# Experts of a decoder layer: running sums on GpSimd, another order of the experts, gathers that skip the padding

## The chip, the cores and the metric

The kernel runs on one core of a Trainium2 chip. Its metric is the device time of one execution in microseconds, as the median of several runs. The engines are TensorE (PE), VectorE (DVE), ScalarE (ACT), GpSimd (POOL) and SyncE (SP); SP issues the loads of weights and lists, GpSimd the indirect gathers and scatters. Times inside an execution are microseconds from the start of its span.

## The reference

One decoder layer for 2048 tokens of 1024 channels: a mixer sub-layer of three head groups, then a sub-layer of experts, then a final RMS norm. Only the experts and the final norm matter here. Each token goes to two of 32 experts (the best of 4 groups, and the two best of its 8 experts), and each expert is a SwiGLU of hidden width 512:

```python
def hier_moe(h, wg, bg, we, be, w_gate, w_up, w_down):
    ...
    weights = grp_p * jax.nn.softmax(top_l, axis=-1)
    expert = grp_i * MOE_EXPERTS_PER_GROUP + top_j
    ...
    def run(inp):
        xb, e = inp
        hid = jax.nn.silu(xb @ w_gate[e]) * (xb @ w_up[e])
        return hid @ w_down[e]
    ...
    contrib = out[dest] * flat_w[order][:, None].astype(out.dtype)
    y = jnp.zeros((T, D), out.dtype).at[tok_sorted].add(contrib)
...
    x = x + gt2 * hier_moe(h, ...)
return rms_norm(x, final_norm_g)
```

## The kernel before

The experts are the last stage of the program, from about 1900 us on. The routing has written, for each expert, a list of its tokens to DRAM (`tab_d`). The experts are worked off as 32 items in an order that the device finds: experts are ranked by how many rows they got, and the item at position p takes the expert of a rank that the list `CAP` stands for. `CAPR` holds the rows set aside for each rank (240, 208, 208, 208, 192, ... 88; 4644 in all, while the routing fills 4096), and `CAP` deals them out to positions:

```python
CAP = [CAPR[p // 2] if p % 2 == 0 else CAPR[31 - p // 2] for p in range(NE)]
```

So even positions hold the large items, falling from 240, and odd ones the small, rising from 88. An item of more than 128 rows is "full": its rows lie in two tiles (of half of them each), and it is computed with weights and inputs split in two parts (`wh`, `wl`: L1907 on ScalarE, L1908 on VectorE), gate and up in two halves of the hidden width (c = 0 and 1, L1957 and L1959), each ended by `ga` (a copy by ScalarE, L1963, and a sum by VectorE, L1964, for each of two PSUM banks m) and by `hid` (L1968, L1969). An item of up to 128 rows is "few": one tile, gate and up as plain fp32 matmuls on unsplit weights (L1931), then four transposes and `hid` (L1941). 18 items are full, 14 few. Positions 0 to 27 alternate (full, few), and the last four are full.

For an item r the program writes, in this order: the first half of gate and up of r (or all of it, if few); `finish` of item r - 2 (the product L2017 and the scatter L2018 to the output); `partial` of r - 1 (the gathers L1992 of what other experts have so far added to the rows, `part`); the first transposes of r + 1's rows (L1884, with `xT`, L1888 and L1889); the gathers L1866 of the rows of r + 2 (`xg`); the down projection of r - 1 (L162 to L164, with its eviction `y`, L1983); the rest of the transposes; the second half of r; and `add` of r - 1: the sum y + part (L2001), its scatter back to DRAM (L2004, `yp_d`), and the final norm's Square (L2009, ScalarE), `sx` (L2010) and a square root in 14 small steps (L61 to L67, VectorE). The sum carries a manual dependency, "products first": it stands behind the last `hid` product of item r in the scheduler's order.

The final rows go out through L2018 from whichever expert comes last for a token; a row index past the last token makes a scatter skip the row. All indirect gathers and scatters are issued by GpSimd, in the order in which they stand on it. A scheduler sets the order on each engine from the program, with a model of its own; within an engine the order is then fixed. Weights come in pieces of 512 KB through 11 buffers (`wraw`), a few item takes eight of them at once.

## Time and profile before

| | us |
|---|---|
| median of 3 runs | 2964.74 (2964.41 to 2969.07) |
| the profiled execution | 2962.22 |
| its span, first to last instruction | 2960.3 |
| mean granted TensorE clock | 0.886 of full speed |

Over the whole span TensorE is busy 2385.6 us (81%), VectorE 2103.6, ScalarE 1346.8 and GpSimd 1010.4. The experts' stage is the last third. Rows of a profile read: start and duration, engine, line of the kernel, operation, output <- inputs, and in brackets how long the engine had stood idle before and what released it. In rows of groups, busy time and mean duration in ns stand behind the bar, then the idle time before them and what ended it.

### The profile page before, as it was taken

What the parts mean: (1) busy time and instruction counts of PE and PEld (TensorE: products, weight loads), DVE (VectorE), ACT (ScalarE), POOL (GpSimd) and SP (SyncE); (2) the same over time, 40 slices, a digit from 0 to 9 for tenths busy, and PEclk for the clock granted to TensorE, in tenths of its full rate; (3) what the DMA queues carried; (4) which work ended last, traced back from release to release, by engine and by line L of the source; (5) the groups of instructions that cost most, each with busy time, mean ns of one, the idle gap of its engine ahead of it and who ended that gap; (6) DMA issues with size and microseconds to landing.
All of it is one profiled execution on the core that took longest, in us unless ns stands there. A gap on an engine that the chain in (4) does not pass through costs nothing. (4 is left out here: it accounts for less than half of the span.)

```text
span 2960.3 us, 38558 instructions
## 1 busy us (share of the span) xinstructions
PE 2385.6 (81%) x12571; PEld 1857.5 (63%) x12571; DVE 2103.6 (71%) x4776; ACT 1346.8 (45%) x2339; POOL 1010.4 (34%) x755
## 2 busy tenths in 40 slices
PE   3989877777567899858897999488889888987894
PEld 3766645776456677646675878465566655655673
DVE  6478867999978854547786566656667766666785
ACT  2568867574122244356665222244444444443452
POOL 2221133436635332155544344213222222323222
PEclk9999967898767979969998999699999989989997
DMA  7222254433331244243323443588888888887871
GB/s 217 86 92 85 79 200 156 112 136 124 106 106 54 83 147 137 67 149 111 112 69 123 152 148 123 151 271 251 263 272 269 258 250 265 253 247 235 260 226 36
DMA packets 372278, 479.41 MB, mean 162 GB/s; under 512 B 84827, under 2 KB 271355, under 8 KB 371813
## 3 DMA queue, kind: packets, MB, share of 16 engines
q1 hardware_dynamic: 334501, 421.83, 45.0%
q0 software_dynamic: 37568, 55.05, 7.0%
q8 instruction: 100, 1.64, 0.2%
q14 instruction: 109, 0.89, 0.1%
HBM read 385.75 MB, written 112.23 MB: 168 GB/s over the span
## 5 line engine op out<-in xcount | busy, mean ns | idle before, releaser
L1908 DVE TENSOR_TENSOR wl<-wraw,wh 128x1024 fp32r<-128x1024 f32 x272 | 329.6, 1221 | 187.0 <-ACT wh L1907 179.1
L1907 ACT ACTIVATE wh<-wraw 128x1024 fp32r<-128x1024 f32 x272 | 286.4, 1055 | 330.9 <-PE pd L164 120.6
L1957 PE MATMUL pg<-xT,wh 128*128 128x416 f32 (+10 forms) x1152 | 324.3, 361 | 18.6 <-DVE xT L1889 11.5
L1931 PE MATMUL pg<-wraw,xT 128*120 128x512 f32 (+9 forms) x448 | 231.0, 679 | 88.1 <-DVE ga__18823 L1964 11.1
L1959 PE MATMUL pg<-xT,wl 128*128 128x208 f32 (+10 forms) x1152 | 283.2, 246 | 0.0
L441 POOL TENSOR_TENSOR xx<-xr,xx 128x1024 fp32r<-128x1024 f32 x64 | 162.7, 2545 | 268.8 <-ACT xx L440 254.7
L1957 PEld LDWEIGHTS pg<-xT,wh 128*128 128x128 f32 x1152 | 223.2, 194 | 24.8 <-DVE xT L1889 14.0
L1931 PEld LDWEIGHTS pg<-wraw,xT 128*120 128x120 f32 (+9 forms) x448 | 88.2, 202 | 222.3 <-issue 120.3
L1959 PEld LDWEIGHTS pg<-xT,wl 128*128 128x128 f32 x1152 | 226.6, 197 | 0.4
L255 DVE SCALAR_TENSOR_TENSOR sb<-rl,iws,sb 128x1024 f32<-128x1024 f32 (+7 forms) x154 | 186.6, 1212 | 33.3 <-ACT rl L254 24.9
L2004 POOL DMA_INDIRECT yp_d<-y,ix x50 | 97.6, 1952 | 309.6 <-DVE y L2001 170.3
L162 PE MATMUL pd<-wh,hid 128*104 128x512 f32 (+17 forms) x400 | 164.8, 412 | 28.2 <-DVE y L1983 15.1
L162 PE MATMUL pp<-xx,w 128*128 128x256 f32 x512 | 153.5, 300 | 22.3 <-ACT ft L487 11.9
L254 ACT ACTIVATE rl<-pi,iwa 128x1024 f32<-128x1024 f32 (+7 forms) x176 | 157.0, 910 | 30.7 <-DVE sb L255 27.7
L163 PE MATMUL pd<-wl,hid 128*104 128x512 f32 (+17 forms) x400 | 161.1, 403 | 0.0
L164 PE MATMUL pd<-wh,hid 128*104 128x512 f32 (+17 forms) x400 | 160.7, 407 | 0.0
L163 PE MATMUL pp<-xx,w 128*128 128x256 f32 x512 | 151.2, 296 | 4.1 <-POOL xx L441 4.1
L164 PE MATMUL pp<-xx,w 128*128 128x256 f32 x512 | 150.3, 295 | 1.9 <-DVE w L177 1.1
L251 PE MATMUL pi<-iks,iqs 128*128 128x512 f32 (+3 forms) x304 | 110.4, 446 | 32.2 <-ACT rl L254 31.2
L162 PE MATMUL pj<-w,xx 128*128 128x512 f32 (+1 forms) x256 | 99.6, 390 | 40.2 <-DVE ot L208 18.9
L1538 DVE CUSTOM_DVE_ANT_0 pr<-ps,mk 128x512 f32<-128x512 f32 (+3 forms) x160 | 94.3, 605 | 47.6 <-PE ps L1537 28.4
L1992 POOL DMA_INDIRECT part<-yp_d,ix x50 | 65.9, 1319 | 178.6 <-DMA yp_d<-y,ix 169.4
(1073 smaller groups left out, 6914.7 us busy)
## 6 DMA issues: line engine op xcount, KB each, us to landing
wraw<-in_exp_w_gate_dram SPq DMA_DIRECT2D x128, 512.0 KB
wraw<-in_exp_w_up_dram SPq DMA_DIRECT2D x128, 512.0 KB
wraw<-in_exp_w_down_dram SPq DMA_DIRECT2D x128, 512.0 KB
xr<-hT_d SPq DMA_DIRECT2D x64, 512.0 KB
w<-in_ada_w_dram SPq DMA_DIRECT2D x64, 256.0 KB
w<-in_ada_w_dram SPq DMA_DIRECT2D x16, 512.0 KB
xi<-in_x_dram SPq DMA_DIRECT2D x16, 512.0 KB
hT_d<-ht SPq DMA_DIRECT2D x16, 512.0 KB
```

Of the source, the lines that this page charges most:

```text
L162: TE.matmul(ps, st[0], mv[0], start=(k == first), stop=False, **kw)
L163: TE.matmul(ps, st[0], mv[1], start=False, stop=False, **kw)
L164: TE.matmul(ps, st[1], mv[0], start=False, stop=(k == last), **kw)
L251: TE.matmul(pi[:, s0:s0 + sl], iqs[:, h, i * P:(i + 1) * P], iks[:, g0 + s0:g0 + s0 + sl], start=True, stop=True)
L254: S.activation(rl[:, :gl], pi[:, :gl], AF.Relu, scale=iwa[:, b, h:h + 1])
L255: V.scalar_tensor_tensor(sb[:, gs], rl[:, :gl], iws[:, b, h:h + 1], (eps if h == 0 else sb)[:, gs], op0=OP.mult, op1=OP.add)
L441: G.tensor_sub(xx[1][-1], xr, xx[0][-1].bitcast(F32))
L1907: S.activation(wh, w, AF.Copy)
L1908: V.tensor_sub(wl, w, wh.bitcast(F32))
L1931: TE.matmul(pgs[a][:C], xT[:, kk], wp[2 * i + a][:, k], start=(kk == 0), stop=(kk == KD - 1))
L1957: TE.matmul(pgs[m], wh[:, k, ws], xT[:, i * 4 + k], start=(i + k == 0), stop=False, skip_group_check=True)
L1959: TE.matmul(pgs[m][:, 0], wl[:, k, ws], xT[:, i * 4 + k, 0], start=False, stop=(i + k == 4), skip_group_check=True)
```

## The change

- `CAP` deals out the ranks in another order: even positions rise from 136 to 240, odd ones fall from 132 to 88. The first five items are full (136, 132, 140, 132, 144), then few and full take turns (128, 148, 128, 152, ...), and the last two are 240 and 88. Four lines that turn a rank into a position follow it.
- The sum y + part is made by GpSimd, without the manual dependency.
- The tiles `xg`, `part` and `sx` are set up once (to 0, 0 and 1) and used in turn; both gathers get a bound, so that indices of padding rows (past the last token) are skipped.
- Where the next two items are both full, the gathers of item r + 2 are issued after the rest of item r's transposes (`late`).

```diff
-    CAP = [CAPR[p // 2] if p % 2 == 0 else CAPR[31 - p // 2] for p in range(NE)]
+    CAP = [CAPR[15 - p // 2] if p % 2 == 0 else CAPR[16 + p // 2] for p in range(NE)]
...
+    xgt, partt = [[mx_.tile([P, D], F32, name=f"{z}{i}", bufs=1) for i in range(3)] for z in ("xg", "part")]
+    sxt = [mx_.tile([P, 2], F32, name=f"sx{i}", bufs=1) for i in range(4)]
+    for t_ in xgt + partt:
+        G.memset(t_, 0.0)
...
-            xg = mx_.tile([P, D], F32, name="xg", bufs=3)
+            xg = turn(xgt)
             G.indirect_dma_start(out=xg[:n], out_offset=None, in_=h2_d[:, :],
-                                 in_offset=bass.IndirectOffsetOnAxis(ap=ix[:n, 0, j:j + 1], axis=0))
+                                 in_offset=bass.IndirectOffsetOnAxis(ap=ix[:n, 0, j:j + 1], axis=0),
+                                 bounds_check=T - 1, oob_is_err=False)
...
-            part = mx_.tile([P, D], F32, name="part", bufs=PB)
+            part = turn(partt)
             G.indirect_dma_start(out=part[:n], out_offset=None, in_=yp_d[:, :],
-                                 in_offset=bass.IndirectOffsetOnAxis(ap=ix[:n, 0, j:j + 1], axis=0))
+                                 in_offset=bass.IndirectOffsetOnAxis(ap=ix[:n, 0, j:j + 1], axis=0),
+                                 bounds_check=T - 1, oob_is_err=False)
...
-            a = V.tensor_add(y[:n], y[:n], part[:n])
-            if after is not None:
-                tc.add_manual_dep(a.ins, after.ins.name, ORDER, reason="products first")
+            G.tensor_add(y[:n], y[:n], part[:n])
...
-        sx = mx_.tile([P, 2], F32, name="sx", bufs=4)
-        V.memset(sx, 1.0)
+        sx = turn(sxt)
...
-            ahead(r + 2)
+
+            late = r + 2 < NE and min(CAP[r + 1], CAP[r + 2]) > P
+            if not late:
+                ahead(r + 2)
...
+            if late:
+                ahead(r + 2)
```

On VectorE, at the second half of gate and up of a full item that has a few item before and behind it: `wl` are splits of weights, `ga` the sums that set PSUM free, `hid` the end of the half, `rs` the steps of the square root. Before:

```order
L1908 TENSOR_TENSOR wl<-wraw,wh 128x1024 x3
L1964 TENSOR_TENSOR ga__23142<-ga__23142,pg_23108 128x176
L1908 TENSOR_TENSOR wl<-wraw,wh 128x1024
L1964 TENSOR_TENSOR ga__23142<-ga__23142,pg_23109 128x176
L1908 TENSOR_TENSOR wl<-wraw,wh 128x1024
L1964 TENSOR_TENSOR ga__23181<-ga__23181,pg_23147 128x176
L1908 TENSOR_TENSOR wl<-wraw,wh 128x1024
L1964 TENSOR_TENSOR ga__23181<-ga__23181,pg_23148 128x176
L1967 TENSOR_TENSOR ga__23142<-ga__23142,ga__23181 128x2x176
L1969 TENSOR_TENSOR hid<-ga__23142,hid 128x2x176
L2001 TENSOR_TENSOR y<-y,part 116x1024
L2010 TENSOR_SCALAR sx<-sx 128x2
```

At the same place after (L1921 is L1908, L1977 is L1964, L2021 is L2010, L2028 is L2017; the few item whose sum is meant has 120 rows):

```order
L1921 TENSOR_TENSOR wl<-wraw,wh 128x1024 x2
L2021 TENSOR_SCALAR sx_18394<-sx_18394 128x2
...
L67 TENSOR_TENSOR rs_y<-rs_y,rs_t 128x2
L1921 TENSOR_TENSOR wl<-wraw,wh 128x1024
L1977 TENSOR_TENSOR ga__23644<-ga__23644,pg_23610 128x176
L64 TENSOR_TENSOR rs_t<-rs_y 128x2
...
L67 TENSOR_TENSOR rs_y<-rs_y,rs_t 128x2
L2028 SCALAR_TENSOR_TENSOR part_18389<-y,rs_y,fgr 120x1024
L1977 TENSOR_TENSOR ga__23644<-ga__23644,pg_23611 128x176
```

The few item's `sx`, its square root and its last product have moved from behind `hid` to the places ahead of the first and between the first two `ga`. ScalarE at the same place, before (L1963 is the copy that begins `ga`, L2009 the Square):

```order
L1907 ACTIVATE wh<-wraw 128x1024 x2
L1963 ACTIVATE ga__22055<-pg_22021 128x176
L1907 ACTIVATE wh<-wraw 128x1024
L1963 ACTIVATE ga__22055<-pg_22022 128x176
...
L1968 ACTIVATE hid<-ga__22055 128x2x176
L2009 ACTIVATE part,sx<-y 108x1024
```

and after (L1920 is L1907, L1976 is L1963, L2020 is L2009, L1954 is L1941, L1946 the few item's first step after its matmuls):

```order
L1920 ACTIVATE wh<-wraw 128x1024
L2020 ACTIVATE part_18389,sx_18394<-y 120x1024
L1920 ACTIVATE wh<-wraw 128x1024
L1976 ACTIVATE ga__22553<-pg_22519 128x160
L1920 ACTIVATE wh<-wraw 128x1024
L1976 ACTIVATE ga__22553<-pg_22520 128x160
...
L1946 ACTIVATE sg<-pg_22640 120x512
L1901 ACTIVATE xT<-pt 128x4x88
L1920 ACTIVATE wh<-wraw 128x1024 x3
L2020 ACTIVATE part_18390,sx_18391<-y 80x1024
L1954 ACTIVATE hid<-pt 128x4x120
```

The few item's Square has moved ahead of the split that stands before the first `ga`, and a full item's first Square ahead of the few item's `hid`. On GpSimd, a pair of items before:

```order
L2004 DMA yp_d<-y,ix_24033 2049x1024
L1992 DMA part<-yp_d,ix_24033 74x1024
L2018 DMA out_dram<-part,ix_24033 2048x1024
L1992 DMA part<-yp_d,ix_24033 74x1024
L1866 DMA xg<-h_d,ix_25080 70x1024 x2
L2004 DMA yp_d<-y,ix_24033 2049x1024 x2
L1992 DMA part<-yp_d,ix_24033 128x1024
L2018 DMA out_dram<-part,ix_24033 2048x1024 x2
L1866 DMA xg<-h_d,ix_25080 66x1024
```

and after (L2015 is the sum, L2016 the scatter L2004, L2005 is L1992, L2029 is L2018, L1878 is L1866):

```order
L2015 TENSOR_TENSOR y<-y,part_18389 112x1024
L2016 DMA yp_d<-y,ix_23485 2049x1024
L2005 DMA part_18390<-yp_d,ix_23485 96x1024
L2005 DMA part_18388<-yp_d,ix_23485 96x1024
L2029 DMA out_dram<-part_18389,ix_23485 2048x1024
L2015 TENSOR_TENSOR y<-y,part_18390 96x1024
L2016 DMA yp_d<-y,ix_23485 2049x1024
L1878 DMA xg_18387<-h_d,ix_24536 104x1024
L2015 TENSOR_TENSOR y<-y,part_18388 96x1024
L1878 DMA xg_18385<-h_d,ix_24536 104x1024
L2016 DMA yp_d<-y,ix_23485 2049x1024
```

Each scatter now has its sum ahead of it, and the two gathers `xg` of a full item have moved from ahead of its predecessor's scatters to between the sums.

## Rows read from the trace of the kernel before

**Rows 1.** Windows: start:end, length, busy us of PE, PEld, DVE, ACT, POOL, clock, DMA.
```profile
2200.00:2300.00 100.00, 93.07 (x461) 66.92 (x460) 76.84 (x156) 45.13 (x72) 23.84 (x20) 0.98 0.86 272
2800.00:2850.00 50.00, 45.68 (x307) 39.88 (x308) 40.51 (x72) 27.69 (x48) 14.28 (x11) 0.90 0.94 270
```

**Rows 2.** Timeline (start, us), PE, first matmul of the first and of the last few item.
```profile
1943.38 1.15 PE L1931 MATMUL pg<-wraw,xT 128*88 128x512 f32 x1 [11.09 <-DVE ga__18823 L1964]
...
2753.63 1.22 PE L1931 MATMUL pg<-wraw,xT 128*128 128x512 f32 x1 [4.79 <-DVE ga__25751 L1964]
```

**Rows 3.** Timeline: start of the last four full items, end of their gate and up, last gather.
```profile
2786.10 0.29 PE L1957 MATMUL pg<-xT,wh 128*128 128x280 f32 x1
...
2912.29 0.23 PE L1959 MATMUL pg<-xT,wl 128*128 128x132 f32 x1
...
2932.86 0.97 POOL L1992 DMA_INDIRECT part<-yp_d,ix  x1 [0.30 <-issue]
```

**Rows 4.** Timeline, start of the few item at 2253.30.
```profile
2248.47 0.75 DVE L1983 SCALAR_TENSOR_TENSOR y<-pd,pl,gt2r 104x512 f32<-104x512 f32 x1
2249.13 2.35 DVE L1908 TENSOR_TENSOR wl<-wraw,wh 128x1024 fp32r<-128x1024 f32 x2
2250.66 1.06 ACT L1907 ACTIVATE wh<-wraw 128x1024 fp32r<-128x1024 f32 x1 [1.34 <-DMA wraw<-in_exp_w_gate_dram]
...
2252.90 0.35 DVE L1964 TENSOR_TENSOR ga__21503<-ga__21503,pg 128x192 f32<-128x192 f32 x1
...
2253.30 3.65 PE L1931 MATMUL pg<-wraw,xT 128*108 128x512 f32 x4 [4.87 <-DVE ga__21503 L1964]
...
2254.54 1.06 ACT L1907 ACTIVATE wh<-wraw 128x1024 fp32r<-128x1024 f32 x1 [2.60 <-DMA wraw<-in_exp_w_gate_dram]
...
2256.77 0.35 DVE L1964 TENSOR_TENSOR ga__21503<-ga__21503,pg 128x192 f32<-128x192 f32 x1
...
2257.17 1.11 PE L1931 MATMUL pg<-wraw,xT 128*108 128x512 f32 x2 [0.22 <-DVE ga__21503 L1964]
```

**Rows 5.** Timeline, start of the few item at 2068.28.
```profile
2060.18 0.74 DVE L1983 SCALAR_TENSOR_TENSOR y<-pd,pl,gt2r 92x512 f32<-92x512 f32 x1
...
2065.63 1.06 ACT L1907 ACTIVATE wh<-wraw 128x1024 fp32r<-128x1024 f32 x1 [4.66 <-DMA wraw<-in_exp_w_gate_dram]
...
2068.28 2.03 PE L1931 MATMUL pg<-wraw,xT 128*100 128x512 f32 x2 [7.89 <-DVE ga__19881 L1964]
...
2069.28 0.36 DVE L1964 TENSOR_TENSOR ga__19881<-ga__19881,pg 128x208 f32<-128x208 f32 x1
```

**Rows 6.** Groups of instructions from 1880 to 2961.
```profile
L1957 PE MATMUL pg<-xT,wh 128*128 128x416 f32 (+10 forms) x1152 | 324.3, 361 | 18.6 <-DVE xT L1889 11.5 <-DVE ga__24556 L1964 6.4 <-DVE ga__18552 L1964 0.7
...
L2017 DVE SCALAR_TENSOR_TENSOR part<-y,rs_y,fgr 104x1024 f32<-104x1024 f32 (+17 forms) x50 | 63.1, 1281 | 0.9
L2001 DVE TENSOR_TENSOR y<-y,part 104x1024 f32<-104x1024 f32 (+17 forms) x50 | 60.6, 1217 | 32.8 <-DMA part<-yp_d,ix 32.3 <-DVE xT L1889 0.5
...
L2009 ACT ACTIVATE part<-y 104x1024 f32<-104x1024 f32 (+17 forms) x50 | 52.8, 1056 | 73.1 <-DVE y L2001 71.3 <-issue 1.9
...
L64 DVE TENSOR_TENSOR rs_t<-rs_y 128x2 f32<-128x2 f32 x96 | 15.4, 161 | 3.0
```

**Rows 7.** Timeline: a VectorE sum alone, and one beside a GpSimd sum.
```profile
1635.88 1.22 DVE L1729 TENSOR_TENSOR x<-x,xb 128x1024 f32<-128x1024 f32 x1
...
1668.62 2.39 POOL L1661 TENSOR_TENSOR ml<-mf,mh 128x1024 fp32r<-128x1024 f32 x1 [2.28 <-ACT mh L1660]
1669.56 2.54 DVE L1729 TENSOR_TENSOR x<-x,xb 128x1024 f32<-128x1024 f32 x1
```

**Rows 8.** DMA queues from 1880 to 2961: packets, MB, share of 16 engines.
```profile
q0 software_dynamic: 36576, 54.92, 19.2%
```

**Rows 9.** Timeline, a few item's `hid` and the down projection that waits for it.
```profile
2281.88 0.51 ACT L1941 ACTIVATE hid<-pt 128x432 fp32r<-128x432 f32 x1
...
2282.45 0.48 PE L162 MATMUL pd<-wh,hid 128*108 128x512 f32 x1 [0.94 <-ACT hid L1941]
```

More of the change, by code (lines that the diff above doesn't have):

```diff
@@ L1778, in body @@
         V.tensor_scalar(pf_[:, 0:1], rc[:, 0:1], 15.5, None, op0=OP.is_gt)
-        V.tensor_scalar(pf_[:, 1:2], rc[:, 0:1], -4.0, 63.0, op0=OP.mult, op1=OP.add)
+        V.tensor_scalar(pf_[:, 1:2], rc[:, 0:1], 4.0, -61.0, op0=OP.mult, op1=OP.add)
         V.tensor_mul(pf_[:, 0:1], pf_[:, 0:1], pf_[:, 1:2])
-        V.scalar_tensor_tensor(rc[:, 0:1], rc[:, 0:1], 2.0, pf_[:, 0:1], op0=OP.mult, op1=OP.add)
+        V.tensor_scalar(rc[:, 0:1], rc[:, 0:1], -2.0, 30.0, op0=OP.mult, op1=OP.add)
+        V.tensor_add(rc[:, 0:1], rc[:, 0:1], pf_[:, 0:1])
         V.tensor_scalar(oh, iota32[0:NE], rc[:, 0:1], None, op0=OP.is_equal)
@@ L1822, in body @@
     mps_ = es.enter_context(tc.tile_pool(name="mps", bufs=1, space=PSUM))
-    YB, PB = 2, 3
+    YB = 2
     TS = 1
@@ L1827, in body, with turn @@
     CM = max(CAP[0::2]), max(P, max(CAP[1::2]))
+    xgt, partt = [[mx_.tile([P, D], F32, name=f"{z}{i}", bufs=1) for i in range(3)] for z in ("xg", "part")]
+    sxt = [mx_.tile([P, 2], F32, name=f"sx{i}", bufs=1) for i in range(4)]
+    for t_ in xgt + partt:
+        G.memset(t_, 0.0)
+    for t_ in sxt:
+        G.memset(t_, 1.0)
+    def turn(tiles):
+        tiles.append(tiles.pop(0))
+        return tiles[-1]
     def load_list(pl, row, C):
@@ L1990, in partial, with add @@
         for j in range(nb):
-            part = mx_.tile([P, D], F32, name="part", bufs=PB)
+            part = turn(partt)
             G.indirect_dma_start(out=part[:n], out_offset=None, in_=yp_d[:, :],
-                                 in_offset=bass.IndirectOffsetOnAxis(ap=ix[:n, 0, j:j + 1], axis=0))
+                                 in_offset=bass.IndirectOffsetOnAxis(ap=ix[:n, 0, j:j + 1], axis=0),
+                                 bounds_check=T - 1, oob_is_err=False)
             parts.append(part)
         return parts
-    def add(st, ys, parts, after=None):
+    def add(st, ys, parts):
         n, nb, pl, ix, xgs = st
         for j, (y, part) in enumerate(zip(ys, parts)):
-            a = V.tensor_add(y[:n], y[:n], part[:n])
-            if after is not None:
-                tc.add_manual_dep(a.ins, after.ins.name, ORDER, reason="products first")
+            G.tensor_add(y[:n], y[:n], part[:n])
             G.indirect_dma_start(out=yp_d[:, :], out_offset=bass.IndirectOffsetOnAxis(ap=ix[:n, 1, j:j + 1], axis=0),
                                  in_=y[:n], in_offset=None, bounds_check=T - 1, oob_is_err=False)
-        sx = mx_.tile([P, 2], F32, name="sx", bufs=4)
-        V.memset(sx, 1.0)
+        sx = turn(sxt)
         for j, (y, part) in enumerate(zip(ys, parts)):
@@ L2093, in body @@
         if r:
-            fin = sts[r - 1], ys, parts, add(sts[r - 1], ys, parts, after)
+            fin = sts[r - 1], ys, parts, add(sts[r - 1], ys, parts)
     finish(*fin)
```

## The prediction

> **What bounds the kernel now.** Only the experts' stage changes, from about 1900 us to the end of the span at 2960.3. I read the table by stretch first: between 2000 and 2800 TensorE is busy 82 to 93 us of each 100, VectorE some 70, ScalarE 45, GpSimd 24 to 32, the DMA engines 0.79 to 0.88 of the time (eight stretches of 100 us, one of them in [rows 1]). TensorE sets the pace, so its waits are what counts. The stage is a chain of equal pairs, one "full" and one "few" item: from the first few item to the fourteenth it is 2753.63 - 1943.38 = 810.2 us, 62.3 per pair [rows 2].
>
> TensorE's one regular wait lies just ahead of every few item (3 to 8 us). The first rows of a few item need the PSUM bank that the full item's second gate half used, so they wait for L1964 (`ga`, first m); their third matmul needs the other bank, so it waits for L1964 (second m). At 2253.30 the order of events is to be seen [rows 4]: ScalarE's split L1907 waits until a gate weight has landed, then the VectorE split, then `ga` 2252.90, then the few item 0.05 us later; the next L1907 again waits 2.60 us for a landing, the second `ga` ends at 2257.12, and the third matmul starts at 2257.17. At 2068.28 the second L1907 does not wait, and the second `ga` ends 1.36 us after the start, before it is needed [rows 5]. So this spot is ended either by a weight's landing or by what stands ahead of `ga` on ScalarE and VectorE.
>
> **The order of the items.** Sizes stay the same; only which one stands where changes. Before: full(0), then 13 pairs, then four full items in a row. After: five full items first, then few and full in turn, the largest full item next to last and the smallest few item last.
> - Head. Full(0) ends its second half at 1943.38 - 11.09 = 1932.3 [rows 2]. Four more full items follow. The only full items in a row that the trace has are the last four, from 2786.10 to 2912.5, 31.6 each [rows 3]. So they end at 1932.3 + 126.4 = 2058.7, and with one gap of 4.8 (the last one) [rows 2] the first few item starts at 2063.5. If the items came at TensorE's own pace (busy 45.68 of the 50 us from 2800 on, so 28.9 an item) [rows 1] it would be 2052.6, with the wait of 11 that the first few item had [rows 2] 2070.
> - Middle: 13 pairs, 810.2 as before, to 2873.7.
> - Tail: after the last few item starts there are that item, a two-tile down projection and a one-tile one. In the trace that stretch is 2753.63 to 2786.10, 32.5 with the next item's transposes [rows 2, 3], say 31.5. From the issue of the last `part` gather to the end it is 2960.3 - 2932.86 = 27.4 [rows 3]; about 1 is added by the slower sum. 60 in all, so 2933.7.
> That is 26.6 us less than 2960.3, with -38 and -20 as bounds: one drain of TensorE at the end of a short item in place of four full items behind the last few one. The zeroing of six tiles on GpSimd stands partly ahead of the routing's last scatters; first gathers of 68 rows in place of 120 give that back: 0, from -1 to +2. The late issue of gathers in the first three items costs nothing as long as it stays a whole item (31.6) ahead of its use.
>
> **Padding rows.** The lists hold 4644 places for 4096 routed rows; both gathers skip 548 each, 1096 x 4096 B = 4.49 MB. The software queue moved 54.92 MB in 19.2% of 16 engines' 1081 us [rows 8], so these are 17 us of all engines. That is the most it can be worth, if DMA were the bound all the time; it is the bound only in part of each pair, so I take -5, and 0 as the other end (a skipped row may still cost its place in the queue).
>
> **Sums on GpSimd.** Removed from VectorE: 50 sums, 60.6 us, and with them 32.3 us in which VectorE stood still for a `part` landing [rows 6]. Where that held back the split of the next item's transposes, TensorE waited 11.5 us for `xT` (L1957) [rows 6]. I take -12 for it, and nothing for the rest, since VectorE isn't the bound. Added: 50 sums of 2.39 us on GpSimd (the sum of two SBUF tiles of this shape at 1668.62) [rows 7], 120 us on an engine busy 30%; in its order each sum stands ahead of its scatter, and the gathers that stood there have moved behind.
>
> The cost is on VectorE and ScalarE, because the wait "products first" has gone. Before, a few item's Square, its 15 small steps of the square root and the L2017 product stood behind the last `hid` of the full item, under the next few item's 16 us of matmuls. The order after puts them around `ga`: on ScalarE Square (1.06 us) [rows 6] ahead of the split that the first `ga` needs; on VectorE seven small steps ahead of the split, and eight (0.19 us each with their spacing) and L2028 (1.28) between the two `ga`: 2.8 us where one split of 1.22 stood. Three waits are new: Square waits for GpSimd, `sx` for Square, `ga` for both.
>
> There is also a contention. Beside a GpSimd sum, VectorE's sum of two SBUF tiles takes 2.54 us, and it ends 1.1 us after GpSimd's; alone it takes 1.22 [rows 7]. The weight split L1908 is of that kind. So each sum holds back a split that starts beside it by up to 2.4 us. The Trainium skill says the same as a rule (SBUF — State Buffer, section "SBUF: two separate sides"): a VectorE instruction with two SBUF inputs and a GpSimd one that reads SBUF take an exclusive lock and the loser blocks; by that rule, moving an addition to GpSimd gives VectorE nothing back where it has splits to do, and the trace agrees (2.54 against 1.22).
>
> Worked at 2253.30 [rows 4]: `y` is ready at 2249.22; the running split ends 2250.35, the sum then takes until 2252.75, Square until 2253.95 with its read-out, the split L1907 (at 2250.66 before) until 2255.0, the VectorE split until 2256.3, `ga` 2256.7: 3.4 later, and the second `ga` 2.8 + 0.4 behind it, 2.8 later than before. At 2068.28 `y` was ready at 2060.92 [rows 5]: sum and Square are over by 2065.7, the first `ga` slips 0.5, the second ends some 2 us later, of which 0.7 was free: 1.8. Two other gaps come out at 3.5 and 2.0 in the same way. I take 2.6, and 14 gaps: +36.4. Farther on, Square of the full item's first tile now stands ahead of the few item's `hid`, for which TensorE already waits 0.94 us [rows 9]: one Square, less what is free, +0.8, 14 times: +11. For clock (0.5 for a few us at longer gaps) and the first half of the next full item I add 0.4 x 14 = +6. Lower bound of all this: 0, if every gap is ended by landings anyway; upper: 14 x 6 = 84, every gap with the full 2.4 of the lock and no cover.
>
> **The sum.** 2933.7 - 5 - 12 + 36.4 + 11 + 6 = 2970.1, +10 on the span; on the profiled run (2962.2) 2972, and since the median of the runs lies 2.5 above that run, 2975.
>
> **Rivals.**
> A, the gap is the landings' (not slower). If the L1907 ahead of each `ga` waits for a weight anyway, Square, the small steps and L2028 lie under that wait, as the 2.60 us at 2254.54 suggest [rows 4]; the later few item then finds its weights there. For it: L1907's waits for landings are frequent. Against it: 8 of 11 weight buffers are held by the few item until it starts, so landings slip with it. It decides when `y` is ready more than 5.5 us ahead of the few item and a landing ends both splits. Then only the 11 for `hid` stay: 2933.7 - 17 + 11 = 2928, 2933 as a median.
> B, the lock decides in the full items too: 36 more sums, two in each, one of which meets the splits for the next first half: 18 x (2.39 - 1.22) = +21: 2996. For it: the 2.54 us beside GpSimd [rows 7]. Against: those splits are several buffers ahead.
> C, padding is the larger part. If DMA sets each pair's pace, the skipped rows give their 17 in place of 5: 2963. If a skipped row costs the same as a read one: 2980.
>
> **How the numbers follow.** Forecast 0.40, A 0.30, B 0.15, C 0.15. A measurement here can tell about 0.2% (6 us) from no change. The forecast's own spread, 2955 to 2990, lies 0.03 faster, 0.10 same, 0.27 slower; A 0.27 faster, 0.03 same; B slower; C 0.06, 0.05, 0.04. That makes 0.36 faster, 0.18 same, 0.46 slower. The range reaches from below A (2926) to above B (3008).
>
> **What would show it.** Right: gaps ahead of few items 2 to 3 us longer, with Square, `sx` and L2028 between the splits and `ga`; a pair at 64 to 66 us; the first few item near 2063; 60 us from the last one to the end; splits of 2.4 us and more beside GpSimd's sums. Wrong: pairs at 62 or less, with L1907 still waiting for landings ahead of each few item (A); long waits for weights in full items (B); less than 2055 or more than 2075 at the first few item breaks the order's term.

## The result, and the profile after

The changed kernel takes 3004.91 us (median of 4 runs, 3001.32 to 3013.86) against 2966.9 for the kernel before on the same chip: ratio 1.0135, 95% interval 1.0105 to 1.0164. It is slower by 38 us. The profiled execution took 3001.39, its span is 2999.6, 39.3 more than before.

By stretches of the span (of the profiled executions, by the starts of TensorE's instructions; the later columns are runs told of below):

| us | before | after | sums on VectorE, behind `hid` | sums on VectorE, early | sums on VectorE, early, steps late |
|---|---|---|---|---|---|
| first full item to first few item | 36.6 | 171.1 | 175.7 | 162.9 | 165.2 |
| first to last few item (13 pairs) | 810.2 | 858.2 | 812.6 | 799.8 | 796.1 |
| last few item to the end | 206.7 | 61.0 | 62.3 | 58.2 | 57.2 |
| sum | 1053.5 | 1090.3 | 1050.6 | 1020.9 | 1018.5 |

Each column is one execution, and such stretches spread from one execution to the next. In the run with the first four sums on GpSimd (below) the 13 pairs take 804.1, though that edit leaves them alone; with all sums on VectorE behind `hid` they take 812.6. So differences of some 8 us between columns say little.

The first and the last few item of the changed kernel, in the timeline (answering [rows 2]):

```profile
2080.42 1.22 PE L1944 MATMUL pg<-wraw,xT 128*128 128x512 f32 x1 [3.44 <-DVE ga__20362 L1977]
...
2938.60 1.09 PE L1944 MATMUL pg<-wraw,xT 128*88 128x512 f32 x2 [1.61 <-DVE ga__27308 L1977]
```

The 13 pairs between them take 66.0 us each, where 62.3 were; that is 48 us. Head and tail together take 232.1 where 243.3 were, 11 less. Two stretches by window (columns as in [rows 1]):

```profile
2200.00:2300.00 100.00, 68.64 (x321) 46.52 (x320) 63.77 (x120) 38.28 (x62) 36.65 (x23) 0.86 0.73 225
2700.00:2800.00 100.00, 85.56 (x444) 66.27 (x443) 71.15 (x114) 46.40 (x70) 40.34 (x26) 0.97 0.72 231
```

TensorE is busy 68.64 and 85.56 us of 100. The first window is the lowest of the nine from 2000 to 2900; the others have 79.9 to 88.2, where 80.6 to 93.1 were before. The run with the order alone (below) has 70.81 in that window, so the low is not the sums' alone. No other engine is near 100. From the first full item to its last matmul TensorE stands still for 178 us, where it was 142, and is busy 886, where it was 883: the loss is in waits. Three groups of the kernel before that [rows 6] doesn't show:

```profile
L1908 DVE TENSOR_TENSOR wl<-wraw,wh 128x1024 fp32r<-128x1024 f32 x272 | 329.6, 1221 | 187.0 <-ACT wh L1907 179.1 <-DMA wraw<-in_exp_w_gate_dram 5.2 <-PE pg L1931 1.2
...
L1931 PE MATMUL pg<-wraw,xT 128*120 128x512 f32 (+9 forms) x448 | 231.0, 679 | 88.1 <-DVE ga__18823 L1964 11.1 <-DVE ga__23142 L1964 8.3 <-DVE ga__19881 L1964 7.9
...
L162 PE MATMUL pd<-wh,hid 128*104 128x512 f32 (+17 forms) x400 | 164.8, 412 | 28.2 <-DVE y L1983 15.1 <-ACT hid L1941 13.1
```

And the groups of the changed kernel (L1921 is L1908, L1970 is L1957, L1944 is L1931, L2015 is L2001, L2020 is L2009):

```profile
L1921 DVE TENSOR_TENSOR wl<-wraw,wh 128x1024 fp32r<-128x1024 f32 x272 | 392.4, 1449 | 148.0 <-ACT wh L1920 141.6 <-DMA wraw<-in_exp_w_gate_dram 5.2 <-PE pt L1897 0.8
L1970 PE MATMUL pg<-xT,wh 128*128 128x352 f32 (+10 forms) x1152 | 335.1, 369 | 35.3 <-DVE xT L1902 23.7 <-DVE ga__24010 L1977 3.5 <-DVE ga__19215 L1977 2.2
L1944 PE MATMUL pg<-wraw,xT 128*120 128x512 f32 (+9 forms) x448 | 225.9, 667 | 107.8 <-DVE ga__21462 L1977 14.7 <-DVE ga__21999 L1977 12.3 <-DVE ga__20908 L1977 10.5
L162 PE MATMUL pd<-wh,hid 128*104 128x512 f32 (+17 forms) x400 | 163.7, 409 | 26.4 <-ACT hid L1954 21.0 <-DVE y L1996 5.4
...
L2015 POOL TENSOR_TENSOR y<-y,part 104x1024 f32<-104x1024 f32 (+17 forms) x50 | 124.9, 2498 | 323.9 <-DVE y L1996 288.8 <-issue 27.3 <-ACT xT L1899 5.8
...
L2020 ACT ACTIVATE part<-y 104x1024 f32<-104x1024 f32 (+17 forms) x50 | 52.9, 1058 | 103.0 <-POOL y L2015 103.0
```

Three things are to be seen. A weight split takes 1449 ns in place of 1221, 62 us over the 272: as much as the 60.6 us of sums that VectorE was freed of. TensorE waits longer at all three spots: ahead of few items 107.8 us (88.1), for the transposes' split `xT` 23.7 (11.5), for the few item's `hid` 21.0 (13.1). (Its wait for the eviction `y` fell, to 5.4 from 15.1.) And ScalarE's Square, each of the 50, waits for GpSimd's sum, 103 us in all; before it waited 71.3 for VectorE's [rows 6].

The longest wait of a few item, in the timeline:

```profile
2201.09 1.93 POOL L2029 DMA_INDIRECT out_dram<-part,ix  x1 [1.71 <-issue]
...
2207.62 0.74 DVE L1996 SCALAR_TENSOR_TENSOR y<-pd,pl,gt2r 128x512 f32<-128x512 f32 x1
...
2210.85 1.36 POOL L2029 DMA_INDIRECT out_dram<-part,ix  x1 [7.84 <-DVE wl L1921]
2212.51 1.08 POOL L1878 DMA_INDIRECT xg<-h_d,ix  x1 [0.30 <-issue]
2213.62 2.35 POOL L2015 TENSOR_TENSOR y<-y,part 128x1024 f32<-128x1024 f32 x1
2216.01 1.06 ACT L2020 ACTIVATE part<-y 128x1024 f32<-128x1024 f32 x1 [7.40 <-POOL y L2015]
...
2217.06 1.04 ACT L1920 ACTIVATE wh<-wraw 128x1024 fp32r<-128x1024 f32 x1
...
2219.65 0.30 DVE L1977 TENSOR_TENSOR ga__21462<-ga__21462,pg 128x152 f32<-128x152 f32 x1
...
2220.00 2.92 PE L1944 MATMUL pg<-wraw,xT 128*124 128x512 f32 x3 [14.74 <-DVE ga__21462 L1977]
```

`y` is ready at 2208.36, but the sum starts at 2213.62: on GpSimd an output scatter stands ahead of it, 9.8 us behind the one before it, and a gather. Square waits 7.40 us for the sum, and with it ScalarE, whose split ahead of `ga` stands behind Square. This gap is the extreme. Over the 13 later few items, whose start has a few item's sum ahead of it, the sum begins 1.6 to 5.3 us behind `y` at six and at most 0.9 us behind it at seven. And a place where GpSimd's sum holds VectorE, in a later pair:

```profile
2645.61 3.84 DVE L1921 TENSOR_TENSOR wl<-wraw,wh 128x1024 fp32r<-128x1024 f32 x1 [0.23 <-ACT wh L1920]
...
2645.97 2.38 POOL L2015 TENSOR_TENSOR y<-y,part 96x1024 f32<-96x1024 f32 x1
...
2649.37 1.01 DVE L1902 TENSOR_TENSOR xT<-pt,xT 128x384 fp32r<-128x384 f32 x2
...
2649.97 0.44 PE L1970 MATMUL pg<-xT,wh 128*128 128x384 f32 x1 [2.17 <-DVE xT L1902]
```

A split that takes 1.22 alone takes 3.84 beside the sum, the `xT` behind it on VectorE comes 2.6 us later, and TensorE waits 2.17. Such waits of some 2.2 us stand ahead of the first half of ten full items.

### The profile page after: what moved, and what is told of

It is laid out like the page before. It is cut to its first block, busy times and chain, and to the rows that moved or that the text cites. A ratio compares the mean times of both kernels' runs of the same rounds, so it can differ in the third digit from the quotient of the medians.

```text
span 2999.6 us, 38641 instructions
## 1 busy us (share of the span) xinstructions
PE 2387.3 (80%) x12563; PEld 1865.6 (62%) x12563; DVE 2125.3 (71%) x4692; ACT 1345.5 (45%) x2337; POOL 1137.9 (38%) x815
## 5 line engine op out<-in xcount | busy, mean ns | idle before, releaser
L1921 DVE TENSOR_TENSOR wl<-wraw,wh 128x1024 fp32r<-128x1024 f32 x272 | 392.4, 1449 | 148.0 <-ACT wh L1920 141.6
L1920 ACT ACTIVATE wh<-wraw 128x1024 fp32r<-128x1024 f32 x272 | 286.0, 1053 | 286.6 <-PE pd L164 91.5
L1970 PE MATMUL pg<-xT,wh 128*128 128x352 f32 (+10 forms) x1152 | 335.1, 369 | 35.3 <-DVE xT L1902 23.7
L1944 PE MATMUL pg<-wraw,xT 128*120 128x512 f32 (+9 forms) x448 | 225.9, 667 | 107.8 <-DVE ga__21462 L1977 14.7
L1972 PE MATMUL pg<-xT,wl 128*128 128x176 f32 (+10 forms) x1152 | 287.5, 250 | 1.5 <-DVE wl L1921 1.5
L1970 PEld LDWEIGHTS pg<-xT,wh 128*128 128x128 f32 x1152 | 229.1, 199 | 45.7 <-DVE xT L1902 29.3
L2015 POOL TENSOR_TENSOR y<-y,part 104x1024 f32<-104x1024 f32 (+17 forms) x50 | 124.9, 2498 | 323.9 <-DVE y L1996 288.8
L1944 PEld LDWEIGHTS pg<-wraw,xT 128*120 128x120 f32 (+9 forms) x448 | 87.6, 200 | 237.4 <-issue 115.9
L2005 POOL DMA_INDIRECT part<-yp_d,ix x50 | 74.1, 1482 | 149.4 <-DMA yp_d<-y,ix 143.6
L2029 POOL DMA_INDIRECT out_dram<-part,ix x50 | 72.5, 1449 | 152.1 <-DMA out_dram<-part,ix 49.4
```

The lines of the kernel that those rows point to most:

```text
L1920: S.activation(wh, w, AF.Copy)
L1921: V.tensor_sub(wl, w, wh.bitcast(F32))
L1944: TE.matmul(pgs[a][:C], xT[:, kk], wp[2 * i + a][:, k], start=(kk == 0), stop=(kk == KD - 1))
L1970: TE.matmul(pgs[m], wh[:, k, ws], xT[:, i * 4 + k], start=(i + k == 0), stop=False, skip_group_check=True)
L1972: TE.matmul(pgs[m][:, 0], wl[:, k, ws], xT[:, i * 4 + k, 0], start=False, stop=(i + k == 4), skip_group_check=True)
L2015: G.tensor_add(y[:n], y[:n], part[:n])
```

## The experiments

Each part of the change was first put in or taken out alone. Ratios are to the kernel before on the same chip, with 95% intervals.

**Sums back on VectorE, behind `hid`, the rest of the change kept.**

```diff
-            G.tensor_add(y[:n], y[:n], part[:n])
+            a = V.tensor_add(y[:n], y[:n], part[:n])
+            if after is not None:
+                tc.add_manual_dep(a.ins, after.ins.name, ORDER, reason="products first")
...
```

> The changed kernel with its sums back on VectorE, behind the last hid of the item as in the kernel before; order of items, late gathers, tiles used in turn and skipped padding stay. Theory (the sums on GpSimd cost all the loss, some 60 us, and order and padding alone gain 20 to 30): 2940, from 2930 to 2950; pair of items 62 us, first few item near 2064. Rival 1 (the new order costs as such: its five full items in a row at the start run at 34.5 us each whoever adds, and the first few item comes at 2080): 2955 to 2970. Rival 2 (sums are not the point, the skipped gathers or the tiles used in turn are): 2990 to 3005, as the changed kernel.

Measured: 2961.38, ratio 0.9984 (0.9969 to 0.9999). The sums' move is the loss, some 43 us of it; but order and padding alone gain 5 us, not 20 to 30. The pairs are back at 62.5 us, and the first few item comes at 2086.6: for this run rival 1 has the head right. (Its "whoever adds" falls below: with early sums on VectorE the head is 13 us shorter.)

**The order of items (with the late gathers) alone, on the kernel before.**

```diff
-    CAP = [CAPR[p // 2] if p % 2 == 0 else CAPR[31 - p // 2] for p in range(NE)]
+    CAP = [CAPR[15 - p // 2] if p % 2 == 0 else CAPR[16 + p // 2] for p in range(NE)]
...
+            late = r + 2 < NE and min(CAP[r + 1], CAP[r + 2]) > P
+            if not late:
+                ahead(r + 2)
...
```

> The kernel before with the new order of items and the late gathers alone. Theory: 2945 (2935 to 2955), that is 22 less than before: first few item near 2064 instead of 1943, then 13 pairs of 62.3, then 60 to the end. Rival 1 (full items in a row at 34.5): 2955 to 2970, first few item at 2075 to 2080, pairs as before. If order and padding add up, e1 minus this run is what padding is worth.

Measured: 2967.58, ratio 1.0013 (0.9993 to 1.0033). The order alone, with the sums late on VectorE, is worth nothing. Four full items less at the end save 143 us of tail; at the start they cost 142 (head 178.9 against 36.6; the profiled execution is 13 us above the run's median, and the run above has 175.7). Padding is then 6 us, by the difference to the run above, which has pairs of 62.5 where this one has 63.1; by the two intervals that is barely clear of nothing.

**Sums on GpSimd alone, on the kernel before.**

```diff
-            a = V.tensor_add(y[:n], y[:n], part[:n])
-            if after is not None:
-                tc.add_manual_dep(a.ins, after.ins.name, ORDER, reason="products first")
+            G.tensor_add(y[:n], y[:n], part[:n])
...
```

> The kernel before with the sums on GpSimd alone, without the dependency that puts them behind hid. Theory: pairs of 66 us in place of 62.3, weight splits on VectorE of 1.45 us mean in place of 1.22, and the four full items at the end longer too: 3015 (3005 to 3030), more than the changed kernel. Rival 2: 2965 to 2975.

Measured: 3024.03, ratio 1.0198 (1.0180 to 1.0215). As the theory had it: pairs of 67.5 (in an execution 14 us above the median), splits of 1451 ns; few items wait 132.1 us, `xT` 29.1. The tail did not grow (206.4). With the sums on GpSimd in both, order and padding together are worth 19 us (1.0135 against 1.0198, give or take 10).

**Padding skipped and tiles used in turn alone.**

```diff
-            xg = mx_.tile([P, D], F32, name="xg", bufs=3)
+            xg = turn(xgt)
...
+                                 bounds_check=T - 1, oob_is_err=False)
...
```

> The kernel before with the tiles used in turn and the padding rows skipped, alone. Theory: 2962 (2952 to 2967). If DMA sets the pace of the pairs: 2950 (17 us less). Rival 2 (tiles used in turn tie gathers to each other): above 2970.

Measured: 2974.3, ratio 1.0018 (1.0000 to 1.0036). The 13 pairs take 800.0, 10 less than before, but the tail 26 more. Without the late gathers, which were left out here, a tile of `xg` is filled again while rows of the last full items have still to be transposed from it (so part of those items' rows are others'), and TensorE waits for gathers at that place. From 2740 to the end, TensorE's waits (total, times, longest):

```profile
PE pt L1896 <- DMA xg<-h_d,ix: 27.5, 3, 15.9
```

So the late gathers belong to the tiles used in turn, and only the pairs are read from this run. They put the padding at up to 10 us, within the spread of single executions.

Then the loss of the sums was taken apart: is it the place of the steps behind them, or GpSimd?

**Sums on VectorE, early (without the dependency).**

```diff
-            G.tensor_add(y[:n], y[:n], part[:n])
+            V.tensor_add(y[:n], y[:n], part[:n])
```

> The changed kernel with the sums on VectorE, but without the dependency that puts them behind hid: the sum, sx, the steps of the root and the last product stand ahead of and between the two ga, as with GpSimd, and there is no GpSimd sum to hold VectorE. The run with the sums on VectorE behind hid took 2961, the changed kernel 3005. Theory place (the steps around ga make the loss): 2990 to 3000, waits of few items some 105 us in all. Theory lock (the sums beside the splits make it): 2963 to 2975, splits at 1.22, waits of few items 80 to 90. My guess is half and half: 2978.

Measured: 2934.7, ratio 0.9902 (0.9877 to 0.9927). That is below both theories: 70 us less than the changed kernel by one changed line, and 28 less than before. Groups:

```profile
L1970 PE MATMUL pg<-xT,wh 128*128 128x352 f32 (+10 forms) x1152 | 322.3, 359 | 8.6 <-ACT wh L1920 4.2 <-DVE ga__20017 L1977 1.4 <-DVE ga__19254 L1977 1.0
L1944 PE MATMUL pg<-wraw,xT 128*120 128x512 f32 (+9 forms) x448 | 227.4, 669 | 95.2 <-DVE ga__21999 L1977 13.1 <-DVE ga__23090 L1977 12.2 <-DVE ga__20908 L1977 11.3
L2015 DVE TENSOR_TENSOR y<-y,part 104x1024 f32<-104x1024 f32 (+17 forms) x50 | 61.0, 1219 | 5.1 <-DMA part<-yp_d,ix 4.4
```

VectorE waits 4.4 us for gathered rows, where it waited 39.2 with the sums behind `hid` (32.3 before, [rows 6]). That fits: an early sum sends its scatter early, so the next item's gather has landed when its sum comes up. TensorE's wait for `xT` is no longer among the first three (under 1.0 us). Few items do wait more (95.2 against 77.5 with the sums behind `hid`), as the prediction had it for steps around `ga`. The head is 162.9: the four added full items take 126.3 us, 31.6 each, where they take 34.8 with the sums behind `hid`.

The steps are not quite where the changed kernel has them, though, as the scheduler ordered the engines anew. ScalarE ahead of the start of the seventh few item (L1920 is the split, L2020 Square, L1976 the copy of the first `ga`), in the changed kernel:

```profile
2478.36 1.06 ACT L2020 ACTIVATE part<-y 120x1024 f32<-120x1024 f32 x1 [3.19 <-POOL y L2015]
...
2479.41 1.04 ACT L1920 ACTIVATE wh<-wraw 128x1024 fp32r<-128x1024 f32 x1
2480.36 0.29 ACT L1976 ACTIVATE ga__23644<-pg 128x176 f32<-128x176 f32 x1
```

And in this run:

```profile
2440.84 1.99 ACT L1920 ACTIVATE wh<-wraw 128x1024 fp32r<-128x1024 f32 x2
2444.02 1.06 ACT L2020 ACTIVATE part<-y 120x1024 f32<-120x1024 f32 x1 [1.19 <-DVE y L2015]
...
2445.07 0.30 ACT L1976 ACTIVATE ga__23644<-pg 128x176 f32<-128x176 f32 x1
```

With GpSimd's sums Square stands ahead of the split that the first `ga` needs, at all of the 13 later few items; with VectorE's it stands behind that split at 11. So the 70 us are the engine and this shift together.

**Sums on GpSimd, steps behind `hid`.**

```diff
-            S.activation(part[:n], y[:n], AF.Square, accum_out=sx[:n, j:j + 1])
+            a = S.activation(part[:n], y[:n], AF.Square, accum_out=sx[:n, j:j + 1])
+            if after is not None:
+                tc.add_manual_dep(a.ins, after.ins.name, ORDER, reason="products first")
...
```

> The changed kernel with its sums on GpSimd, and Square (so also sx, root and last product) put behind the last hid of the item by a dependency of order. Theory place: 2960 to 2972, few items' waits back to 80. Theory lock: 2985 to 3005, splits still at 1.45 mean, transposes' splits still late (24 us of waits for xT). Guess: 2980. If this run and the one with early steps on VectorE each lose about half, the two add up; if both lose nearly all, each alone uncovers the same wait.

Measured: 2988.18, ratio 1.0096 (1.0068 to 1.0124). The time lies in the range of the theory of the lock. It is about 12 us less than the changed kernel, near the edge of what the intervals tell. Few items wait 83.8, but `xT` more than ever:

```profile
L1921 DVE TENSOR_TENSOR wl<-wraw,wh 128x1024 fp32r<-128x1024 f32 x272 | 381.6, 1407 | 177.6 <-ACT wh L1920 169.8 <-DMA wraw<-in_exp_w_gate_dram 7.0
L1970 PE MATMUL pg<-xT,wh 128*128 128x352 f32 (+10 forms) x1152 | 340.5, 373 | 40.7 <-DVE xT L1902 34.6 <-ACT wh L1920 3.2 <-DVE ga__19254 L1977 1.8
```

The waits for `xT` are not the changed kernel's, though. A place of 2.62, one of ten alike among the 13:

```profile
2577.00 2.48 POOL L1878 DMA_INDIRECT xg<-h_d,ix  x1 [0.30 <-DVE hid L1955]
...
2579.50 2.40 POOL L2015 TENSOR_TENSOR y<-y,part 88x1024 f32<-88x1024 f32 x1
2581.93 1.06 ACT L2020 ACTIVATE part<-y 88x1024 f32<-88x1024 f32 x1 [3.81 <-POOL y L2015]
...
2582.99 0.47 ACT L1901 ACTIVATE xT<-pt 128x384 fp32r<-128x384 f32 x1
...
2583.66 0.55 DVE L1902 TENSOR_TENSOR xT<-pt,xT 128x384 fp32r<-128x384 f32 x1
...
2584.26 0.44 PE L1970 MATMUL pg<-xT,wh 128*128 128x384 f32 x1 [2.62 <-DVE xT L1902]
```

Here `y` is ready at 2576.45, and a gather stands ahead of the sum on GpSimd; the sum begins 3.05 us behind `y` (3.0 to 4.5 at the ten). Square waits for the sum, and ScalarE's last copy of `xT` stands behind Square. That is the queue and the longer sum. A split held to 4.2 us stands ahead of `xT` at two of the other three places, one of 2.8 at the last.

**Spare sums on GpSimd in the kernel before.**

```diff
+    scr = mx_.tile([P, 352], F32, name="scr", bufs=1)
...
+            for q in range(3):
+                G.tensor_add(scr[:n], part[:n, q * 320:q * 320 + 352], fgr[:n, 0:352])
             a = V.tensor_add(y[:n], y[:n], part[:n])
```

> The kernel before, with three spare sums of 352 columns on GpSimd for every gathered tile (they read the gathered tile and a constant, and their result is not used); everything else as before, so the splits alone can meet them. 150 sums of about 0.9 us, 130 us on GpSimd. Theory lock: splits at 1.35 to 1.45 mean, 2990 to 3010. Theory place: 2966 to 2975, and what is lost comes from scatters that start up to 2.7 us later.

Measured: 3010.64, ratio 1.0166 (1.0144 to 1.0187). In size this is what the lock should give, but not in kind: the splits take only 1278 ns (15 us in all), while Square, which overwrites the gathered tile, waits 83.4 us for the spare sums (here by source line):

```profile
L2003 POOL TENSOR_TENSOR scr<-part,fgr x150: 916/948/4261, 1906.9 to 2976.8; 104x352 f32<-104x352 f32 x24, 88x352 f32<-88x352 f32 x21, 120x352 f32<-120x352 f32 x15, 96x352 f32<-96x352 f32 x12
...
  ACT part L2012: 83.4, 20
```

So the run doesn't tell lock from queue; it shows that work on GpSimd which nobody needs costs 48 us.

**The first four items' sums on GpSimd, all others on VectorE behind `hid`.**

```diff
-            a = V.tensor_add(y[:n], y[:n], part[:n])
-            if after is not None:
+            a = (G if gp else V).tensor_add(y[:n], y[:n], part[:n])
+            if after is not None and not gp:
+                tc.add_manual_dep(a.ins, after.ins.name, ORDER, reason="products first")
...
```

> The changed kernel with the sums of the first four items (the full items in a row) on GpSimd and their steps behind hid, all others on VectorE behind hid. It asks whether VectorE's wait for the gathered rows (39 us in the run with all sums on VectorE) is what makes full items in a row slow. If so: first few item 4 to 8 us earlier than with all sums on VectorE (2087 there), 2953 to 2958. If not: 2960 to 2966.

Measured: 2953.22, ratio 0.9958 (0.9938 to 0.9978). The head is 172.1 where it was 175.7 with all sums behind `hid`: VectorE's wait in the full items in a row is part of their length, no more. GpSimd's own hold on the splits is in this head, however; early sums on VectorE take it to 162.9, and to 165.2 with the steps late.

The last four runs ask what it is about GpSimd, and what the best form is.

**Writes in place of the sums on GpSimd** (the sum is left out).

```diff
-            G.tensor_add(y[:n], y[:n], part[:n])
+            G.memset(part[:n, 0:512], 1.0)
+            G.memset(y[:n], 1.0)
+            G.memset(y[:n], 1.0)
```

> The changed kernel with each GpSimd sum replaced by GpSimd writes that read nothing: 512 columns of the gathered tile and twice the tile y are set to 1.0, together about 2.4 us, with the same waits before (y and the gathered tile) and behind (Square and scatter). The sum itself is left out, so the experts' contributions are not in the output. GpSimd is as busy and the chain behind y as long as with the sum; only the reading of two SBUF tiles beside VectorE's splits is gone. Theory lock (VectorE held at its splits makes the loss): splits 1.22 again, 2925 to 2945, as with early sums on VectorE (2935). Theory queue (2.4 us on GpSimd instead of 1.2 on VectorE, ahead of scatters and Square): 2985 to 3005, splits 1.22.

Measured: 2990.39, ratio 1.0087 (1.0058 to 1.0116). Groups (L2022 is the Square):

```profile
L1970 PE MATMUL pg<-xT,wh 128*128 128x352 f32 (+10 forms) x1152 | 334.9, 369 | 26.1 <-DVE ga__19986 L1977 6.8 <-DVE ga__19254 L1977 4.2 <-DVE ga__19602 L1977 3.0
L1921 DVE TENSOR_TENSOR wl<-wraw,wh 128x1024 fp32r<-128x1024 f32 x272 | 331.1, 1221 | 150.0 <-ACT wh L1920 145.8 <-DMA wraw<-in_exp_w_gate_dram 3.5 <-PE pg L1972 0.3
...
L1944 PE MATMUL pg<-wraw,xT 128*120 128x512 f32 (+9 forms) x448 | 232.8, 682 | 122.9 <-DVE ga__22031 L1977 17.5 <-DVE ga__21488 L1977 17.2 <-DVE ga__23134 L1977 12.6
...
L2022 ACT ACTIVATE part<-y 104x1024 f32<-104x1024 f32 (+17 forms) x50 | 52.9, 1058 | 114.1 <-POOL y L2017 114.1
```

All 272 splits are back at 1221 ns and `xT` is no longer among the first three waits (under 3.0 us), so both came from GpSimd's reading beside VectorE. Yet only 14 of the 70 us come back. Few items wait 122.9, 15 us more than in the changed kernel, and Square 114.1. In part that is the queue, as at the same place as above:

```profile
2228.37 1.37 POOL L2031 DMA_INDIRECT out_dram<-part,ix  x1 [7.34 <-DMA out_dram<-part,ix]
2230.05 1.08 POOL L1878 DMA_INDIRECT xg<-h_d,ix  x1 [0.30 <-issue]
2231.13 0.97 POOL L2016 MEMSET y<- 128x1024 f32 x1
2232.16 0.95 POOL L2017 MEMSET y<- 128x1024 f32 x1
2233.14 1.06 ACT L2022 ACTIVATE part<-y 128x1024 f32<-128x1024 f32 x1 [12.04 <-POOL y L2017]
...
2236.94 2.06 PE L1944 MATMUL pg<-wraw,xT 128*124 128x512 f32 x2 [17.17 <-DVE ga__21488 L1977]
```

Here the wait is named: the output scatter waits for the landing of the one before. One reserve: the writes wait for the gathered rows and for `y` in two pieces, and Square waits 11 us more than in the changed kernel. So this run has waits of its own; and its order on ScalarE has a full item's first Square behind the few item's `hid`, where the changed kernel has it ahead. The 14 us are therefore no clean price of the reading. At nine of the 13 later few items the last write begins 1.1 to 2.2 us behind `y`, of which about 1 is the write ahead of it; the queue shows at the other four (4.3 to 11.3).

**Each sum twice on VectorE, early** (the gathered rows are added two times).

```diff
-            G.tensor_add(y[:n], y[:n], part[:n])
+            V.tensor_add(y[:n], y[:n], part[:n])
+            V.tensor_add(y[:n], y[:n], part[:n])
```

> The changed kernel with the sums on VectorE, without the dependency, and each sum made twice (the gathered rows are added two times, so the output is another). VectorE then gives 2.4 us to each sum, as much as GpSimd's lock can take from it, and the chain behind y is as long as with GpSimd; scatters and gathers stay free of GpSimd work. With each sum once it was 2935. If VectorE's time at these places and the length of the chain make the loss: 2975 to 3005. If the loss needs GpSimd (its queue, or a lock that falls elsewhere): 2938 to 2955.

Measured: 2948.97, ratio 0.9939 (0.9911 to 0.9968). 61 us more work on VectorE and a chain as long as GpSimd's cost about 11 us, against 70 on GpSimd. So the length of the operation is the smaller part, as far as this run can tell: here Square stands behind the split at 11 of the 13 later few items, and at seven behind the copy of the first `ga` too, so the longer chain had less to hold up.

**The kernel before without the dependency, and nothing else.**

```diff
-            a = V.tensor_add(y[:n], y[:n], part[:n])
-            if after is not None:
-                tc.add_manual_dep(a.ins, after.ins.name, ORDER, reason="products first")
+            V.tensor_add(y[:n], y[:n], part[:n])
```

> The kernel before without the dependency that puts the sums behind hid, and nothing else. Theory (order of items and padding are worth nothing together, as the run with the order alone, 2967, and with both, 2961, say; early sums are the gain of the run at 2935): 2935 to 2948, VectorE's waits for gathered rows down from 32 to about 5 us. Rival (the gain needs the new order, since early sums help full items in a row): 2955 to 2967.

Measured: 2964.64, ratio 0.9998 (0.9977 to 1.0020): the rival. In the old order early sums gain nothing (few items wait 116.2 us, which takes back what `xT` and `y` give). Order and padding with early sums are worth 28 us (0.9902 against 0.9998), with late ones 5.

**Sums on VectorE early, steps behind `hid`.**

```diff
-            G.tensor_add(y[:n], y[:n], part[:n])
+            V.tensor_add(y[:n], y[:n], part[:n])
...
+                tc.add_manual_dep(a.ins, after.ins.name, ORDER, reason="products first")
...
```

(the dependency on Square, as in the run with GpSimd's steps late).

> The changed kernel with the sums on VectorE, free to stand early, but Square (so sx, root, last product) behind the last hid of the item. Theory (early sums free scatters and gathers, early steps cost the few items' start): few items' waits from 95 back to 80, 2915 to 2928. If the steps around ga lie under landings anyway: 2930 to 2940. If the gain of 26 us came from early Square and product, through the output scatters, and not from the early sums: 2950 to 2962.

Measured: 2928.72, ratio 0.9863 (0.9843 to 0.9883), below both kernels: 37 us under the one before, and by the ratios some 80 under the changed one. Its groups (of an execution 11 us above the median, most of that ahead of the experts' stage):

```profile
L1970 PE MATMUL pg<-xT,wh 128*128 128x352 f32 (+10 forms) x1152 | 324.3, 361 | 12.9 <-ACT wh L1920 5.0 <-DVE ga__21284 L1977 2.2 <-DVE ga__19254 L1977 1.6
L1944 PE MATMUL pg<-wraw,xT 128*120 128x512 f32 (+9 forms) x448 | 224.7, 663 | 79.8 <-DVE ga__21999 L1977 11.7 <-DVE ga__23090 L1977 9.6 <-DVE ga__24161 L1977 7.9
L162 PE MATMUL pd<-wh,hid 128*104 128x512 f32 (+17 forms) x400 | 163.6, 409 | 24.0 <-ACT hid L1954 12.3 <-DVE y L1996 11.7
```

With the changed order and padding, the four runs make a square:

| ratio to before | steps behind `hid` | steps around `ga` |
|---|---|---|
| sums early on VectorE | 0.9863 | 0.9902 |
| sums on GpSimd | 1.0096 | 1.0135 |

The engine costs 2.3% (70 us) in both columns, the place of the steps 0.4% (12 us, with intervals of 0.2 to 0.3% to either side) in both rows; as far as that tells, the two add.

What the 70 are made of differs by column, and part of it is the scheduler's doing. With steps behind `hid`, few items' waits hardly grow with the engine (83.8 against 79.8) and those for `hid` not at all (12.3); the first halves' wait for `xT` is 34.6 against 1.4. At ten of 13 places it comes by GpSimd's queue and its longer sum, as shown above, with ScalarE's last copy of `xT` behind the Square that waits; with early sums on VectorE that copy stands ahead of the second Square. With steps around `ga`, `xT` is 23.7 against 0.3, `hid` 21.0 against 6.5 and few items 107.8 against 95.2. There ten of the waits for `xT` are the held splits, and the rest mixes GpSimd's queue, its longer sum and the shifted Square. Besides, TensorE's matmuls take 14 to 18 us longer with GpSimd's sums, at a mean granted clock of 0.91 in the stage, where it is 0.92 with VectorE's.

So it is shown that the sums on GpSimd, with the order that the scheduler then makes, cost 70 us, and the traces show a held split, a queue and a longer sum at work. How the 70 divide among them is not shown. Two runs give hints: 14 us come back without the reading of two SBUF tiles, and 11 are the length of the sum, each in a run with another order on ScalarE.

## Why the prediction was right and wrong

It said slower, 2975, and gave 3008 as the upper end; it is slower, at 3005, with four times the loss forecast on the span (39 against 10). The direction came from a mechanism that the trace has in part. That the time still lies inside the range is luck: the upper end was set to lie above rival B, and two misses that the forecast did not foresee carried the time close to it. The runs price the two halves of the sum. Order and padding, forecast -31.6, are worth 19 with the sums on GpSimd (1.0135 against 1.0198). The sums, forecast 41.4 (-12 + 36.4 + 11 + 6), cost 58 in the old order (1.0198).

- **Order, forecast -26.6: the first step that failed.** First few item 2063.5 forecast, 2080.4 measured, past the 2075 that was to break this term; last few item to the end 60 and 61.0. Head and tail together gave 11. Four full items were priced at 31.6 each, from the start of the first to the end of the last one's gate and up [rows 3]. That stretch leaves out the last down projection and the drain behind it. The same four items cost 206.7 - 60 = 147 in the forecast's own tail, 36.7 each: so moved to the head they cost what they save, as the run with the order alone shows (1.0013). But what an item in a row costs hangs on the sums, for which the forecast had no step: with early sums on VectorE the four take 31.6 to 32.2 each at the head in three runs, about the price that was forecast, and order and padding together are worth 28 (0.9902 against 0.9998); with GpSimd's sums they take 33.6 in the changed kernel, with late ones on VectorE 34.8.
- **Padding, forecast -5:** 6 by one difference and 10 by another, neither well clear of the spread. Rival C's 17 is not borne out; that a skipped row saves nothing is not excluded.
- **Pairs, forecast 36.4 more in all with padding and `xT` in it:** 48. The wait ahead of few items grew by 19.7 (36.4 forecast), `hid` by 7.9 (11 forecast). **`xT`, forecast -12, is the second step that failed.** It rose by 12, and by 18 with the sums alone: taking the sums off VectorE did remove its wait for gathered rows, but GpSimd's sums hold the splits that stand ahead of `xT`. The contention was in the working, priced at the few item's gap alone; its waits fell on full items (rival B's mechanism, at about half of its price).
- **Steps around `ga`:** in the trace as forecast, and 12 us by the square, with the sums on either engine. The forecast's 41.4 for the sums is near the 43 us between the changed kernel and the one with sums behind `hid`, but for other reasons. What the forecast left out is the queue: the sum was worked as if nothing stood ahead of it on GpSimd (`y` at 2249.22, its start at 2250.35); GpSimd's order, shown ahead of it, has an output scatter and a gather there. Output scatters wait for the landing of the one before, in seven of the 50 in the changed kernel (49.4 us) and in eleven before (67.9), where no sum stood behind them. "An engine busy 30%" was no ground to leave that out; what it costs in all is not shown. (Over the 13 later few items Square begins 56 us behind `y` in sum, and 57 with early sums on VectorE; so at this place the queue alone is not it.)
- **The lock rule** (Trainium skill, SBUF — State Buffer, "SBUF: two separate sides"): the trace agrees that two-input operations of both engines exclude each other, 1449 against 1221 ns a split and 1221 again with writes that read nothing. Its price was taken at the few item's gap alone; in the changed kernel it shows at `xT`, in ten waits of some 2.2 us.
- **Rival A** (landings cover it) is refuted: few items wait longer in every run with GpSimd's sums, or with steps around `ga`, than in its twin without. With the steps late the difference is 4 us (83.8 against 79.8).

One reading is off without harm: from 2000 to 2800 the least that TensorE is busy is 80.6 us of 100, not 82.

## What to carry to other kernels

An engine that is busy a third of the time can still be a bad place for work on a chain. Look at whose operations its reading holds up, along the whole chain and not at one gap (here the splits ahead of `xT`). Look also at what stands ahead of it in that engine's order, and what that waits for (here scatters that wait for the landing of the one before). When one line changes, compare the orders of all engines before the difference is put down to that line. To price a moved piece, take the whole difference that its presence makes at the place where it stands, drain and all, not its pitch between two of its own starts. And try the simplest form of the same idea on its own: an early sum on the same engine, with the steps that nobody waits for left late, gave 37 us where the move to another engine lost 38.

## What had not been expected of the hardware

A VectorE split whose record begins 0.36 us ahead of GpSimd's sum was still the one held back (3.84 us, above), and the sum was not (2.38). So it is with 14 splits of the changed kernel, whose records begin 0.34 to 0.89 us ahead of a sum and which take 3.8 to 4.4 us. Six that begin 0.2 us ahead, and two that begin 0.7 and 0.9 us ahead, end in 1.22, and the sum beside them takes 2.5 to 3.3. So the starts of the records don't tell which of the two will be held.
